# Three jobs of w_down's partial sums in DRAM get later places in the plan of the weights

## The chip, the cores and the metric

The kernel runs on one core of one Trainium2 chip. The metric is the device time of one execution in microseconds (us), lower is better. Three executions of the kernel before gave 869.16 to 869.73 us, median 869.48. A fourth execution was profiled and took 867.14 us; the trace in it spans 865.4 us from the first to the last instruction. All times "at" some microsecond are counted from the start of that span.

## What is computed

One encoder layer on 512 tokens of width 1024, in float32. Shortened:

```
n    = rms_norm(x);  proj = n @ w_in          # u | zu | zv | gate_a | gate_b
ga, gb = sigmoid(gate_a), sigmoid(gate_b)
ya   = s5(u); ya = ya * sigmoid(ya @ w_glu)   # bidirectional state-space scan
yb   = gelu(zu) * spatial_mix(layer_norm(gelu(zv)))
h    = x + (ga * (ya @ w_proj_a) + gb * (yb @ w_proj_b)) @ w_out
h    = h + cross_attention(rms_norm(h), rms_norm(mem); w_q, w_k, w_v, w_xo)
h    = h + (silu(f @ w_gate) * (f @ w_up)) @ w_down      # f = rms_norm(h)
out  = rms_norm(h)
```

## The kernel before

**Products.** Every float32 operand is split into a rounded high part and a remainder, and a product is three matmuls (high by high, high by low, low by high). The split of a weight block is one cast on ScalarE (`whi`, L85) and one subtraction on VectorE (`wlo`, L86). The tiles `whi` and `wlo` have three buffers each, and so has `raw`, into which SyncE loads a block from DRAM.

**Seven products for eight.** The matrices of the second gate (gb), of w_q, w_gate, w_up and w_down are cut into 2 by 2 quarters, and seven products of sums of quarters replace eight products of quarters. The products are numbered 1 to 7. The sums of weight quarters are made in three ways. For the second gate they are formed in SBUF, in the tile `gw`: loads by SyncE, additions on VectorE, and additions by transfers that GpSimd issues with `accum_op=ALU.add` (L261, L267). For w_q and w_down they are prepared in DRAM, in `qsum` and `dsum`: a *job* is a copy of one block of the weight into `dsum`, issued by SyncE (L316), and the addition of a second block onto it, issued by GpSimd (L317). There are 32 jobs: 0 to 7 for w_q, 8 to 31 for w_down. Jobs 8 to 13 are the six chunks of product 5's sum. `dsum` is read only at the end of the kernel (L330), and as the second operand of later jobs.

**The plan.** `plan` is the list of all weight blocks in the order in which the matmuls use them. Around the change its entries are: 28 to 35 w_proj_b; 36 to 49 the second gate, fourteen products in the order of `ORDER` (two column halves i = 0 and 1: 1, 1, 2, 2, 5/0, 6/0, 5/1, 7/0, 6/1, 4/0, 7/1, 3/0, 4/1, 3/1, written as product/half); 50 and 51 w_glu; 52 to 55 w_proj_a; 56 to 63 w_out; 64 to 71 w_k. `next_w` is called once for each entry, right before its matmuls are written down. At entry i it issues the loads of later entries, each with its own lead (`LOADS` = 3 entries for most), and the splits of entries up to i + 2. A job is hung on two entries: its copy on entry j and its addition on entry j + step, both with a lead of 0, so that they are written down when `next_w` reaches these entries.

**The order in the queues** is not the order in which the instructions are written down. A scheduling pass at build time simulates the kernel and lays out a fixed queue for each engine; at run time each queue is worked off in order, and an instruction that waits holds up those behind it. `tc.keep_in_program_order` (L316) binds an instruction to come somewhere behind the one that was written down for the same engine just before it. The copies of the jobs carry it, the additions don't. So the copy of the job at place 50 comes behind the load of entry 52, and the copy at place 52 behind the last of the four loads of `gat` (L1452), which are written down between w_glu and w_proj_a.

**The second gate, half 0, where it touches `gw`** (`plan_gates`, lines 233 to 270). The tile t of half 0 holds the operand of products 5 and 6; when product 6 has been split (cast and subtraction read t), GpSimd issues `t += b(1, 0)` (L261), and the result is the operand of product 4. The PSUM bank gx takes products 1, 6, 7 and 4 of a half, one onto the other, and is read out after 1, 6, 7 and 4; the read-out after 7 is `kept(gx[i], "u3")`, a copy on ScalarE (L1313). So product 4 of half 0 waits for the cast and the subtraction of its weights, and for that copy.

```
elif q == 6:
    nc.vector.tensor_tensor(b11, t, b11, ALU.subtract)
    nc.gpsimd.dma_start(t, b(1, 0), accum_op=ALU.add)
```

Of the kernel before, what the change touches and what calls it, by code (L numbers as in the profile page):

```python
# [52 lines left out]
def hybrid_layer_kernel(  # L53
# [160 lines left out]
    def query_block(i, j, n):  # L214
        return block(w_q, i * KD // 2, KD // 2, 512 * n + 256 * j, 256)
# [78 lines left out]
    def down_block(i, jc, c):  # L294
        row, k = (4 * c + 2 * i, 2) if c < CHUNKS - 1 else (NF - 2 + i, 1)
        return block(w_down, row, k, 512 * (1 - jc), 512)

    def down_sum(q, c):
        return dsum[q][:, 2 * c:min(2 * c + 2, NF // 2), :]

    def plan_sums(places):


        jobs = []
        for q, first, more in ((5, (0, 0), lambda n: query_block(0, 1, n)), (7, (0, 1), lambda n: query_block(1, 1, n)),
                               (6, None, lambda n: query_block(1, 1, n)), (4, None, lambda n: query_block(1, 0, n))):
            for n in range(2):
                jobs.append((qsum[q, n], qsum[q + (-1 if q == 6 else 2), n] if first is None else query_block(*first, n),
                             more(n)))
        for q, i, jc, more in ((5, 0, 0, lambda c: down_block(0, 1, c)), (7, 0, 1, lambda c: down_block(1, 1, c)),  # L310
                               (6, 1, 1, lambda c: down_sum(5, c)), (4, 1, 0, lambda c: down_sum(6, c))):
            for c in range(CHUNKS):
                jobs.append((down_sum(q, c), down_block(i, jc, c), more(c)))
        assert len(jobs) == len(places)
        for (dst, src, more), (j, step) in zip(jobs, places):
            plan[j][1].append((0, lambda d=dst, x=src: tc.keep_in_program_order(nc.sync.dma_start(d, x))))  # L316
            plan[j + step][1].append((0, lambda d=dst, x=more: nc.gpsimd.dma_start(d, x, accum_op=ALU.add)))  # L317
# [44 lines left out]
    for i in range(4):  # L362
# [4 lines left out]
    plan_down(w_down, lambda q, c: down_tokens[0](q, c), down_plan)  # L367
    plan_units(UNITS, down_plan)

    plan_sums([(5 + 3 * i, 3) for i in range(8)] + [(50 + 2 * i, 2) for i in range(7)] +  # L370
              [(85 + 3 * i, 3) for i in range(3)] + [(122 + 5 * i, 4) for i in range(14)])
    used_w = [0]

# [1661 lines left out]
```

## Time and profile before

| | |
|---|---|
| median of three executions | 869.48 us (869.16 to 869.73) |
| the profiled execution | 867.14 us |
| its span | 865.4 us |
| mean granted TensorE clock | 0.996 |
| DMA | 155.40 MB in 110135 packets |

In rows of a timeline the columns are start, length, engine, line of the kernel, operation, output<-inputs, how many, and in brackets how long the engine stood idle before and what ended that. "SPq" is SyncE's queue, PE is TensorE, DVE VectorE, ACT ScalarE, POOL GpSimd. In rows of windows each engine has its busy time and its count of instructions; then come the granted TensorE clock, the mean busy share of the 16 DMA engines and GB/s. In rows of DMA issues the last number is the time from issue to landing.

### The profile page before, as it was taken

The page shows a single profiled execution, that of the slowest core. Times are in us where ns is not written, and L with a number is a line of the kernel's source. Part 1 is how long each engine was busy: PE and PEld are TensorE (multiplying, and loading weights), DVE is VectorE, ACT ScalarE, POOL GpSimd, SP SyncE. Part 2 cuts the span into 40 slices and gives each one's busy share as a digit, 9 for nine tenths or more (in the row PEclk, how much of TensorE's full clock was granted, in tenths as well). Part 3 has the DMA queues.
Part 4 walks back from the last instruction along what each step waited for, and adds up shares of the span by engine and source line. Part 5 has one row for each costly group of instructions (what it writes and reads, how often), then busy time and mean ns, then how long its engine had stood idle before and what let it go on. Part 6 is the DMA issues. An engine that isn't in the chain of part 4 may idle for free.

```text
span 865.4 us, 14842 instructions
## 1 busy us (share of the span) xinstructions
PE 853.9 (99%) x5898; PEld 761.9 (88%) x5898; DVE 648.2 (75%) x890; ACT 475.1 (55%) x703; POOL 103.5 (12%) x157
## 2 busy tenths in 40 slices
PE   9999999999999899999999999999999999999996
PEld 6788888878889888889899888999999999988885
DVE  6699589957947658669658646767877768899876
ACT  6645774377436534557547544645545555656664
POOL 1001144100611010110010001001111111000000
PEclk9999999999999999999999999999999999999999
DMA  8559279645638586944687144557799789686641
GB/s 260 159 144 240 81 204 267 147 122 162 167 98 226 136 224 202 287 116 169 200 269 216 68 145 105 146 140 177 172 224 230 204 208 240 178 243 203 196 158 48
DMA packets 110135, 155.40 MB, mean 180 GB/s; under 512 B 8985, under 2 KB 77105, under 8 KB 110002
## 3 DMA queue, kind: packets, MB, share of 16 engines
q1 hardware_dynamic: 91762, 128.27, 45.3%
q0 software_dynamic: 18016, 25.66, 18.4%
q8 instruction: 46, 0.75, 0.3%
q10 hardware_dynamic: 288, 0.52, 0.2%
q14 instruction: 23, 0.19, 0.1%
HBM read 148.70 MB, written 37.20 MB: 215 GB/s over the span
## 4 chain that ended last, share of the span: by engine, by line
PE 96%; ACT 1%; DVE 1%; issue 1%; POOLq 0%; POOL 0%; ACTq 0%
PE pf L404 25%; PE pt L404 18%; PE px L1304 13%; PE dx L404 6%; PE pq L1304 6%; PE dq L404 3%; PE pv L1304 3%; PE gx L1304 3%; PE qx L1304 3%; PE dv L404 2%; PE ptr L577 1%; PE psc L404 1%; PE gq L1304 1%; PE po L404 1%; PE py L1093 1%; PE qq L1304 1%
## 5 line engine op out<-in xcount | busy, mean ns | idle before, releaser
L85 ACT CAST whi<-wraw 128x1024 fp32r<-128x1024 f32 x132 | 135.8, 1029 | 143.3 <-PE pf L404 37.2
L86 DVE TENSOR_TENSOR wlo<-wraw,whi 128x1024 fp32r<-128x1024 f32 x132 | 157.5, 1194 | 66.0 <-ACT whi L85 65.7
L404 PE MATMUL pf<-xn,whi 128*128 128x512 f32 x320 | 100.4, 393 | 0.0
L1304 PE MATMUL px<-fn,whi 128*128 128x256 f32 x480 | 83.3, 276 | 0.0
L1304 PEld LDWEIGHTS px<-fn,whi 128*128 128x128 f32 x480 | 72.5, 188 | 0.2
L404 PEld LDWEIGHTS pf<-xn,whi 128*128 128x128 f32 x320 | 59.6, 188 | 12.6 <-issue 0.5
L85 ACT CAST whi<-b 128x1024 fp32r<-128x1024 f32 x40 | 42.1, 1054 | 51.5 <-PE px L1304 26.3
L86 DVE TENSOR_TENSOR wlo<-b,whi 128x1024 fp32r<-128x1024 f32 x40 | 48.9, 1224 | 27.9 <-ACT whi L85 27.9
L1304 PE MATMUL px<-fn,wlo 128*128 128x256 f32 x240 | 66.4, 277 | 0.0
L404 PE MATMUL pf<-xn,wlo 128*128 128x512 f32 x160 | 62.9, 393 | 0.0
L1304 PE MATMUL pq<-s,whi 128*128 128x256 f32 x320 | 55.0, 276 | 0.0
L404 PE MATMUL dx<-whi,s 128*128 128x512 f32 x170 | 53.0, 390 | 0.0
L86 DVE TENSOR_TENSOR wlo<-t,whi 128x1024 fp32r<-128x1024 f32 x30 | 36.7, 1225 | 19.3 <-ACT whi L85 19.3
L85 ACT CAST whi<-t 128x1024 fp32r<-128x1024 f32 x30 | 31.6, 1052 | 35.2 <-PE pv L1304 12.6
L1304 PEld LDWEIGHTS pq<-s,whi 128*128 128x128 f32 x320 | 48.2, 188 | 0.0
L1304 PEld LDWEIGHTS px<-fn,wlo 128*128 128x128 f32 x240 | 45.1, 188 | 0.0
L1304 PE MATMUL pq<-s,wlo 128*128 128x256 f32 x160 | 44.2, 276 | 0.0
L404 PE MATMUL pt<-whi,xn 128*128 128x512 f32 x120 | 40.1, 402 | 0.0
L404 PEld LDWEIGHTS dx<-whi,s 128*128 128x128 f32 x170 | 31.8, 188 | 6.7 <-DVE s L86 0.3
L317 POOL DMA_DIRECT2D dsum<-in_w_down_dram x12 | 13.3, 1108 | 192.1 <-DMA dsum<-in_w_down_dram 192.1
L404 PEld LDWEIGHTS pf<-xn,wlo 128*128 128x128 f32 x160 | 30.1, 188 | 6.1 <-issue 0.2
L404 PE MATMUL dx<-wlo,s 128*128 128x512 f32 x85 | 33.0, 390 | 0.1
(485 smaller groups left out, 2340.0 us busy)
## 6 DMA issues: line engine op xcount, KB each, us to landing
wraw<-in_w_in_dram SPq DMA_DIRECT2D x34, 512.0 KB, 6.1
dsum<-in_w_down_dram SPq DMA_DIRECT2D x20, 512.0 KB, 6.4
wraw<-dsum SPq DMA_DIRECT2D x20, 512.0 KB, 3.7
b<-in_w_gate_dram SPq DMA_DIRECT2D x15, 512.0 KB, 5.1
b<-in_w_up_dram SPq DMA_DIRECT2D x15, 512.0 KB, 5.2
wraw<-in_w_down_dram SPq DMA_DIRECT2D x15, 512.0 KB, 4.7
dsum<-in_w_down_dram POOLq DMA_DIRECT2D x10, 512.0 KB, 7.3
dsum<-dsum POOLq DMA_DIRECT2D x10, 512.0 KB, 7.1
```

The costliest lines, as they stand in the source:

```text
L85: hi = nc.scalar.copy(dst_hi, src)
L86: lo = nc.vector.tensor_tensor(dst_lo, src, dst_hi.bitcast(F32), ALU.subtract)
L317: plan[j + step][1].append((0, lambda d=dst, x=more: nc.gpsimd.dma_start(d, x, accum_op=ALU.add)))
L404: last_mm[0] = nc.tensor.matmul(ps, a[x], b[y], start=start and i == 0, stop=stop and i == 2, skip_group_check=free)
L577: tr = nc.tensor.transpose(ps[:, j, :], src[:, k * P:(k + 1) * P], ident)
L1093: in_order(nc.tensor.matmul(ps[64 * j:64 * j + 64, :], a, b, start=g % 4 == k == 0, stop=k == 2, tile_position=(0, 64 * j), skip_group_che ...
L1304: nc.tensor.matmul(ps[:, j, :], a[x], b[y], start=start and j == k == i == 0, stop=k == 3 and i == 2, skip_group_check=True)
```

## The change

The places of jobs 8 to 14 are written out instead of computed. The step to the addition stays 2.

```diff
-    plan_sums([(5 + 3 * i, 3) for i in range(8)] + [(50 + 2 * i, 2) for i in range(7)] +
+    plan_sums([(5 + 3 * i, 3) for i in range(8)] + [(j, 2) for j in (53, 54, 55, 56, 58, 60, 62)] +
               [(85 + 3 * i, 3) for i in range(3)] + [(122 + 5 * i, 4) for i in range(14)])
```

Jobs 8, 9 and 10 (chunks 0, 1 and 2 of product 5's sum) go from places 50, 52 and 54 to 53, 54 and 55, their additions from 52, 54 and 56 to 55, 56 and 57. Jobs 11 to 14 keep 56, 58, 60 and 62. What is computed is the same.

## The prediction

> **What bounds the kernel now.** I read the page first, then the waits of TensorE, then the timelines of the engines around its one long wait.
>
> ```profile
> PE 853.9 (99%) x5898; PEld 761.9 (88%) x5898; DVE 648.2 (75%) x890; ACT 475.1 (55%) x703; POOL 103.5 (12%) x157
> ```
>
> TensorE is busy for 853.9 of 865.4 us. An edit that changes no arithmetic can only give back what TensorE waits, or what it loses at a lower clock. All its waits are these, from the view of waits:
>
> ```profile
> PE gx L1304 <- ACT u L1313: 2.4, 1, 2.4
> PE idle L612 <- DVE level L880: 1.1, 1, 1.1
> PE pt L483 <- ACT whi L656: 1.0, 1, 1.0
> PE pf L404 <- DVE yb_lo L86: 0.2, 1, 0.2
> ```
>
> L612, L483 and the yb_lo wait lie in code far ahead of the moved places. The first, half of the total, lies in the second gate. The timelines of TensorE, ScalarE, GpSimd and VectorE there:
>
> ```profile
> 284.21 0.28 PE L1304 MATMUL gx<-gse,wlo 128*128 128x256 f32 x1
> 286.93 0.39 PE L1304 MATMUL gx<-xn,whi 128*128 128x256 f32 x1 [2.45 <-ACT u L1313]
> ```
>
> ```profile
> 277.32 0.58 ACT L1404 COPY u<-gx 128x512 f32<-128x512 f32 x1
> 284.40 1.99 ACT L85 CAST whi<-gw 128x1024 fp32r<-128x1024 f32 x2 [6.51 <-PE gx L1304]
> 286.30 0.58 ACT L1313 COPY u<-gx 128x512 f32<-128x512 f32 x1
> ```
>
> ```profile
> 272.63 1.20 POOL L317 DMA_DIRECT2D dsum<-in_w_down_dram  x1 [31.20 <-DMA dsum<-in_w_down_dram]
> 273.99 1.35 POOL L261 DMA_DIRECT2D gw<-in_w_in_dram  x1 [0.16 <-issue]
> 278.96 1.28 POOL L261 DMA_DIRECT2D gw<-in_w_in_dram  x1 [3.62 <-DVE wlo L86]
> ```
>
> ```profile
> 270.65 2.40 DVE L86 TENSOR_TENSOR wlo<-gw,whi 128x1024 fp32r<-128x1024 f32 x2
> ...
> 277.44 1.23 DVE L86 TENSOR_TENSOR wlo<-gw,whi 128x1024 fp32r<-128x1024 f32 x1 [0.39 <-ACT whi L85]
> ```
>
> And the view of DMA issues in three narrow windows, at 215.8 (an earlier addition onto gw, L267, with GpSimd's queue of transfers empty), at 273.99 and at 278.96:
>
> ```profile
> gw<-in_w_in_dram POOLq DMA_DIRECT2D x1, 512.0 KB, 6.1
> ```
>
> ```profile
> gw<-in_w_in_dram POOLq DMA_DIRECT2D x1, 512.0 KB, 10.3
> ```
>
> ```profile
> gw<-in_w_in_dram POOLq DMA_DIRECT2D x1, 512.0 KB, 7.9
> ```
>
> TensorE waits from 284.49 (284.21 + 0.28) to 286.93 for the copy of u on ScalarE, which ends at 286.88. That copy reads the result of product 7, but it stands third in ScalarE's queue, behind two casts that start at 284.40. The row blames gx of TensorE for the 6.51 us before them. I don't follow it. The first of the two casts makes the weights of product 4 of half 0 from `gw`, and the addition that completes them, the first row of L261, landed at 273.99 + 10.3 = 284.3. The second addition landed at 278.96 + 7.9 = 286.9, after both casts had begun, so it can't be the one.
>
> So the late thing is the first L261, for two reasons. It was issued late: GpSimd stood for 31.20 us at the addition of a job, waiting for its copy, and L261 came 0.16 us after that addition had been issued. And it took 10.3 us behind the job's 512 KB in GpSimd's one queue of transfers, against 6.1 alone.
>
> **Which job that is.** SyncE's queue:
>
> ```profile
> 265.00 1.49 SPq L1452 DMA_DIRECT2D gat<-gad  x1
> 266.53 0.60 SPq L316 DMA_DIRECT2D dsum<-in_w_down_dram  x1
> ...
> 296.97 0.37 SPq L141 DMA_DIRECT2D wraw<-in_w_proj_a_dram  x1
> 297.39 0.58 SPq L316 DMA_DIRECT2D dsum<-in_w_down_dram  x1
> 299.44 6.02 SPq L141 DMA_DIRECT2D wraw<-in_w_proj_a_dram  x3
> 310.39 0.37 SPq L141 DMA_DIRECT2D wraw<-in_w_out_dram  x1
> 310.81 0.56 SPq L316 DMA_DIRECT2D dsum<-in_w_down_dram  x1
> ...
> 315.82 0.37 SPq L141 DMA_DIRECT2D wraw<-in_w_out_dram  x1
> 317.68 0.34 SPq L525 DMA_DIRECT2D g_x<-in_xattn_norm_g_dram  x1
> 318.06 0.56 SPq L316 DMA_DIRECT2D dsum<-in_w_down_dram  x1
> ```
>
> A copy is bound behind what was written down for SyncE just before it. Job 8 (place 50) is bound to the load of entry 52, the first of w_proj_a: the copy at 297.39. Job 9 (place 52) is bound to the last `gat`, and these loads are hoisted far ahead: the copy at 266.53, right behind it. So job 9, not job 8, reaches into the gate. Job 10 (bound to the load of entry 56) is the copy at 310.81, job 11 the one at 318.06.
>
> **The change part by part.** *Copies.* Job 8 at place 53 is bound to the load of entry 55, the last of w_proj_a, which ends at 305.46 (299.44 + 6.02). Job 9 at 54 is bound to the load of entry 56 (310.39), job 10 at 55 to that of 57 (315.82). No job is bound to `gat` any more, and nothing of L316 can come into SyncE's queue ahead of 305.46. Each copy costs 0.56 to 0.60 us of that queue. Behind the load of 55 it stands idle until 310.39; behind that of 56 the present job 10 has the same place; behind that of 57 there are 1.49 us (316.19 to 317.68). All three fit: 0 us. Without that cover a load behind them would come 0.6 us later.
>
> *Additions.* Each takes 1.20 us of GpSimd and follows its copy. Behind 305.46 they come after both L261. L261 then waits only for the subtraction that reads t, the first of the two at 270.65, which ends at 271.85. The second L261 shows the lag: 277.44 + 1.23 = 278.67, issued at 278.96, 0.29 later. So the first is issued at 272.14 instead of 273.99, **1.85 us earlier**.
>
> *Landing.* The trace has no transfer of this kind at this place with the queue empty. Bounds: 6.1 us (alone) and 10.3 us (itself, with the job's transfer ahead). I take 7.9, since the second L261 shared the engines with the end of the first, as the first will with other loads. It lands at 280.0 (bounds 278.2 and 282.4). When must it? From the first cast's start to the end of u's copy ScalarE needs 286.88 - 284.40 = 2.48 us, and TensorE comes free at 284.49: until 282.0. At 280.0 **the whole wait of 2.45 us goes**; at the upper bound 0.6 us of it stay (2.45 - 1.85).
>
> *Clock.* Two windows behind the wait (the granted clock is the third figure from the end):
>
> ```profile
> 288.20:291.70 3.50, 3.50 (x19) 3.50 (x18) 1.97 (x3) 1.19 (x3) 0.00 (x0) 0.51 0.25 80
> 291.70:300.00 8.30, 8.30 (x72) 8.30 (x72) 6.06 (x8) 4.73 (x7) 0.00 (x0) 1.00 0.31 99
> ```
>
> For 3.5 us after the wait the granted clock is 0.51. The loss is 0.49 x 3.50 = **1.7 us**. Bounds: 0, if the dip is not due to the wait, and 1.7. I take 1.7, because the dip begins 1.3 us after the only wait of such length, and because the clock is 1.00 after it. The Trainium skill, "TensorE: Matmul & The Clock Gate", section "HAM oscillation — how this bites in real kernels", speaks against this: by it TensorE's clock is cut by idle gaps over about 3.4 us, and this gap is 2.45. By that rule the dip would be no part of the gain; it is a rival below.
>
> *What is late next.* Product 4 of half 1, from the second L261. In the chain of waits it starts here:
>
> ```profile
> 297.18 2.86 PE gx L1304 x24
> ```
>
> 4.2 us earlier that is 293.0. Its weights land by 286.9 and need a cast and a subtraction, 1.05 (the cast of this kind takes 0.95 to 1.05) and 1.23 us: 289.2, 3.8 us of room.
>
> *The stage that gets the jobs.* Between 297 and 330 jobs 8, 10 and 11 are issued now; job 9 is added, two transfers of 512 KB.
>
> ```profile
> 310.00:320.00 10.00, 10.00 (x46) 8.29 (x45) 6.94 (x8) 3.80 (x6) 1.14 (x1) 1.00 0.75 245
> 320.00:330.00 10.00, 10.00 (x46) 8.29 (x45) 6.31 (x9) 3.40 (x5) 1.13 (x1) 1.00 0.76 196
> ```
>
> At 196 GB/s, the slower of these, 1.05 MB are 5.4 us of the DMA engines; in the 25 us from 305 to 330, at a share of about 0.75, some 6 us are free. TensorE is fully busy here and waits for nothing. So 0 us; the upper bound is 5.4 us, if all of it fell on a load that TensorE waits for (870.7 in the end, counted with the slower case below), and no gain is to be had, as there is no wait to shorten. I take 0, since the work fits into the free share.
>
> **Sum** against the profiled execution's own 867.14: -2.45 - 1.7 = -4.2, that is 862.9. The three runs shown have their median 2.34 us above it, 869.48, and I carry that difference over: **865.3 us**.
>
> **Rivals.**
>
> *The wait goes only in part, or the dip stays.* If the transfer still takes 10.3 us, 1.85 us are gained and 0.6 of waiting stays: 867.6 with the dip, 865.9 without. If the wait goes and the dip stays, as the skill's rule would have it: 2.45 gained, 867.0. For it: the transfer also shared the engines with other loads. Against: any transfer of up to 9.8 us (272.14 to 282.0) takes the whole wait away, and the dip stands right behind the wait.
>
> *The change doesn't do what it says:* 869.5. Either the 6.51 us were TensorE's after all, as the row says, or the scheduling pass, whose queues are laid out anew, puts one new wait of the same size elsewhere. For it: few waits are left because the order happens to fit, and any moved transfer shifts the simulated times behind it. Against: the sum 273.99 + 10.3 meets the cast's start to 0.1 us.
>
> *Slower: GpSimd's waiting moves to the norm of mem.* Three rows of GpSimd, VectorE and TensorE:
>
> ```profile
> 347.07 0.56 POOL L548 TENSOR_TENSOR r<-ms,mhalf 128x1 f32<-128x1 f32 x1 [5.24 <-DVE ms L547]
> 353.16 1.16 POOL L317 DMA_DIRECT2D dsum<-in_w_down_dram  x1 [5.53 <-DMA dsum<-in_w_down_dram]
> ```
>
> ```profile
> 347.67 0.75 DVE L563 SCALAR_TENSOR_TENSOR mt<-mt,r,g_mem 128x512 f32<-128x512 f32 x1 [0.69 <-POOL r L548]
> ```
>
> ```profile
> 352.28 0.60 PE L577 MATMUL ptr<-ident,mt 128*128 128x128 f32 x4
> ```
>
> If the new order puts the addition at 353.16 ahead of r, r starts at 354.3 instead of 347.07, 7.2 us late. On VectorE the scaling of mt waits for r, and everything queued behind it waits too; on TensorE the transposes of mt wait for the scaling. It ends at 348.42 now, 3.9 us ahead of the transposes at 352.28, so the stall is between 3.3 us, by the transposes, and 7.2, if something in VectorE's queue is needed without delay; I take the middle, 5.3, and 1.7 for a new dip: -4.2 + 7.0 = +2.8, **872.3**. It is slower from the point where such a stall exceeds 2.5 us (4.2 - 1.7). For it: the four additions now follow each other closely in this queue. Against: the job at 353.16 (place 58) is not moved, and r stands ahead of it now; the additions of jobs 8 to 11 end near 330, as the last of them still follows the copy at 318.06.
>
> **How the numbers follow.** Forecast 0.63, with a range of its own from 864.4 to 866.6; the partial case 0.13 (to 867.6); no effect 0.14; slower 0.10. A measurement of this kernel can tell about 0.2%, 1.7 us, from no change, so the first two are faster, 0.76, the third the same, 0.14, the last slower, 0.10. The first two hold too little for 8 in 10, so the range reaches into the third: 864.4 to 869.6.
>
> **What would show it.** Right: no addition of L317 between 240 and 300 in GpSimd's timeline; the first L261 near 272.1, landing 6 to 9 us later; ScalarE's two casts apart, the first near 280; no wait of gx in TensorE's list; a granted clock of 1.00 up to the end; copies of L316 behind the loads near 305, 311 and 316, each minus what was gained. Wrong: L261 early and landed early, and the cast still at 284.4 (then TensorE's row was right); a new wait in TensorE's list; r of L548 behind an addition.

## The result, and the profile after

| | before | after |
|---|---|---|
| median | 869.88 us (869.16 to 870.82, 6 runs) | 865.26 us (863.08 to 865.90, 6 runs) |
| profiled execution | 867.14 us | 864.86 us |
| its span | 865.4 us | 863.1 us |

TensorE's busy time on the page of after:

```profile
PE 854.4 (99%) x5898; PEld 762.3 (88%) x5898; DVE 647.5 (75%) x890; ACT 475.2 (55%) x703; POOL 103.5 (12%) x157
```

It is 854.4 of 863.1 us, where it was 853.9 of 865.4: the same instructions, with less time between them. The ratio on record is 0.9944, with a 95% interval from 0.9931 to 0.9957: faster by 0.56%. The medians differ by 4.6 us, the two profiled executions by 2.3 us only. The chain of waits of each shows where the rest went. Before:

```profile
278.88 5.50 PE gx L1304 x47
...
302.78 32.66 PE pf L404 x144
```

And after:

```profile
280.81 8.46 PE gx L1304 x72
...
300.51 32.66 PE pf L404 x144
```

Both pieces named gx begin with product 7 of half 0, and both pieces named pf with the first product behind the second gate. The way between them takes 23.90 us before and 19.70 after: **4.2 us less, the sum of the prediction**. From pf to the end of the span it is 562.6 us in both. But the profiled execution of after came to product 7 1.93 us later. That is a difference of the first 15 us, read here in one window of both. Before, then after (the granted clock is the third figure from the end):

```profile
7.45:14.27 6.82, 5.81 (x32) 4.07 (x30) 5.89 (x11) 5.32 (x11) 0.55 (x1) 1.00 1.05 351
```

```profile
7.45:14.27 6.82, 6.17 (x20) 4.58 (x19) 5.27 (x9) 4.01 (x9) 0.95 (x1) 0.50 1.07 357
```

At half the clock TensorE got through 20 matmuls in place of 32. The change touches nothing there, and in the other kernels below product 7 begins anywhere from 278.9 to 282.4 us. So times in the gate are compared counted from product 7. One of all the executions told of below, of the kernel with more work at the start, was granted a clock of 0.556 throughout, took 1435.54 us and is left out.

The waits of TensorE after:

```profile
PE idle L612 <- DVE level L880: 1.1, 1, 1.1
PE pt L483 <- ACT whi L656: 0.6, 1, 0.6
PE pf L404 <- DVE yb_lo L86: 0.2, 1, 0.2
```

The wait of gx, 2.4 us before, is gone, and no new one stands in the list. GpSimd's timeline, the issue of the first L261, VectorE's and ScalarE's timelines:

```profile
239.43 4.22 POOL L975 DMA_DIRECT2D tt<-kd  x8 [1.65 <-DMA kd<-ks]
274.94 1.37 POOL L261 DMA_DIRECT2D gw<-in_w_in_dram  x1 [31.29 <-issue]
280.90 1.31 POOL L261 DMA_DIRECT2D gw<-in_w_in_dram  x1 [4.59 <-DVE wlo L86]
308.86 1.16 POOL L317 DMA_DIRECT2D dsum<-in_w_down_dram  x1 [26.65 <-DMA dsum<-in_w_down_dram]
...
344.92 0.56 POOL L548 TENSOR_TENSOR r<-ms,mhalf 128x1 f32<-128x1 f32 x1 [5.37 <-DVE ms L547]
350.90 1.16 POOL L317 DMA_DIRECT2D dsum<-in_w_down_dram  x1 [5.42 <-DMA dsum<-in_w_down_dram]
```

```profile
gw<-in_w_in_dram POOLq DMA_DIRECT2D x1, 512.0 KB, 6.0
```

```profile
272.57 2.40 DVE L86 TENSOR_TENSOR wlo<-gw,whi 128x1024 fp32r<-128x1024 f32 x2
274.89 0.68 DVE L1379 TENSOR_TENSOR part<-part,gs 128x512 f32<-128x512 f32 x1
```

```profile
281.00 1.05 ACT L85 CAST whi<-gw 128x1024 fp32r<-128x1024 f32 x1 [1.18 <-DMA gw<-in_w_in_dram]
283.86 1.05 ACT L85 CAST whi<-gw 128x1024 fp32r<-128x1024 f32 x1 [1.81 <-PE gx L1304]
284.82 0.58 ACT L1313 COPY u<-gx 128x512 f32<-128x512 f32 x1
```

No addition of a job stands between the batch of tt and the two L261. The first lands at 274.94 + 6.0 = 280.9, and the cast follows at 281.00. The two casts that stood together at 284.40 are now 1.8 us apart, and the copy of u, third behind them, finds its product when it gets to run. The norm r at 344.92 still stands ahead of the addition at 350.90.

The gate's stretch and SyncE's queue behind it:

```profile
280.90:300.40 19.50, 19.50 (x169) 19.50 (x168) 13.14 (x15) 11.37 (x15) 1.30 (x1) 1.00 0.50 124
```

```profile
294.69 8.49 SPq L141 DMA_DIRECT2D wraw<-in_w_proj_a_dram  x4
303.23 0.61 SPq L316 DMA_DIRECT2D dsum<-in_w_down_dram  x1
308.11 0.38 SPq L141 DMA_DIRECT2D wraw<-in_w_out_dram  x1
308.54 0.58 SPq L316 DMA_DIRECT2D dsum<-in_w_down_dram  x1
...
313.96 0.57 SPq L316 DMA_DIRECT2D dsum<-in_w_down_dram  x1
```

TensorE is busy for all of the 19.50 us, at a clock of 1.00. The copies of jobs 8, 9 and 10 come right behind the loads of entries 55, 56 and 57.

### The profile page after: what moved, and what is told of

Its sections match the earlier page's. It is cut to its first block, busy times and chain, and to the rows that moved or that the text cites. A ratio compares the mean times of both kernels' runs of the same rounds, so it can differ in the third digit from the quotient of the medians.

```text
span 863.1 us, 14838 instructions
## 1 busy us (share of the span) xinstructions
PE 854.4 (99%) x5898; PEld 762.3 (88%) x5898; DVE 647.5 (75%) x890; ACT 475.2 (55%) x703; POOL 103.5 (12%) x157
## 4 chain that ended last, share of the span: by engine, by line
PE 95%; ACT 1%; DVE 1%; DMA 1%; issue 1%; SPq 0%; POOLq 0%; POOL 0%; ACTq 0%
PE pf L404 25%; PE pt L404 18%; PE px L1304 13%; PE dx L404 6%; PE pq L1304 6%; PE dq L404 3%; PE pv L1304 3%; PE gx L1304 3%; PE qx L1304 3%; PE dv L404 2%; PE ptr L577 1%; PE psc L404 1%; PE po L404 1%; PE py L1093 1%; PE qq L1304 1%; PE gq L1304 1%
```

## The experiments

"Start" is the start of product 7 of half 0, "gate" the time from there to the first pf, both read from TensorE's timeline. The profiled time is that of the execution that was traced; where more were timed, the median follows, and the ratio on record to the kernel before on the same chip, with its 95% interval (it is not the quotient of the two medians).

| kernel | profiled | start | wait of gx | gate | median; ratio |
|---|---|---|---|---|---|
| before | 867.14 | 278.95 | 2.45 | 23.67 | 869.88 |
| after | 864.86 | 280.88 | none | 19.47 | 865.26; 0.9944 [0.9931, 0.9957] |
| job 9 alone moved | 864.87 | 280.94 | none | 19.47 | 864.87; 0.9962 [0.9941, 0.9983] |
| jobs 8 and 10 alone | 869.79 | 281.50 | 2.47 | 23.64 | 867.49; 0.9994 [0.9978, 1.0011] |
| addition bound | 865.50 | 281.60 | none | 19.47 | 864.86; 0.9958 [0.9942, 0.9975] |
| two jobs in the gate | 872.36 | 281.43 | 4.94 | 26.47 | 872.79; 1.0050 [1.0030, 1.0069] |
| job between the two L261 | 863.08 | 278.91 | none | 19.47 | one execution |
| wait without transfer | 863.27 | 279.11 | none | 19.69 | one execution |
| transfer without wait | 867.76 | 279.12 | 3.00 | 24.12 | one execution |
| more work at the start | 866.61 | 282.41 | none | 19.47 | 864.87; 0.9955 [0.9938, 0.9973] |
| after, again | 865.82 | 281.80 | none | 19.47 | 865.42; 0.9959 [0.9943, 0.9975] |
| before, again (1) | 869.49 | 281.41 | 2.35 | 23.52 | one execution |
| before, again (2) | 867.10 | 279.29 | 1.86 | 23.08 | one execution |
| before, again (3) | 865.60 | 279.06 | 2.06 | 21.81 | one execution |

The first four experiments have 20 runs of before beside them, with a median of 867.56 us; the two with more work at the start and after again have 21, with 867.85. The three kernels with one execution each have one of before, 865.15 us, and before again has one, 869.85; against the spread of the starts a single time says little, and these kernels are read by their gate.

### Which of the three jobs

Job 9 alone, and then the other two alone:

```diff
-    plan_sums([(5 + 3 * i, 3) for i in range(8)] + [(50 + 2 * i, 2) for i in range(7)] +
+    plan_sums([(5 + 3 * i, 3) for i in range(8)] + [(j, 2) for j in (50, 53, 54, 56, 58, 60, 62)] +
```

> Only job 9 (the copy that stood right behind the last gat load) gets its later place, 53; jobs 8 and 10 stay at 50 and 54. Theory (GpSimd's queue: the addition of job 9 holds up the first addition onto gw, and its transfer goes ahead of it): the whole gain, 4.2 us off the run before, ratio about 0.995; no L317 on GpSimd between 240 and 300; no wait of gx on TensorE; the stretch from product 7 of half 0 to the first matmul of w_glu about 19.7 us, as after, against 23.9 before. Rival (what counts is that all three jobs leave, or the new order of the queues): the gain is less than half, ratio above 0.9975.

```diff
-    plan_sums([(5 + 3 * i, 3) for i in range(8)] + [(50 + 2 * i, 2) for i in range(7)] +
+    plan_sums([(5 + 3 * i, 3) for i in range(8)] + [(j, 2) for j in (53, 52, 55, 56, 58, 60, 62)] +
```

> Jobs 8 and 10 get their later places, 53 and 55; job 9 stays at 52. Theory: no gain, ratio 0.999 to 1.001, the wait of 2.4 us on gx and the half clock behind it are still there, the stretch is 23.9 us. Rival (spreading the traffic, or the new order): a part of the gain, ratio at or below 0.9975.

With job 9 alone moved the gate takes 19.47 us, to the hundredth what the whole change gives. With the other two moved it keeps its 23.64. The waits of TensorE and the timeline of GpSimd in the second kernel:

```profile
PE gx L1304 <- ACT u L1313: 2.5, 1, 2.5
```

```profile
275.05 1.20 POOL L317 DMA_DIRECT2D dsum<-in_w_down_dram  x1 [30.91 <-DMA dsum<-in_w_down_dram]
276.42 1.35 POOL L261 DMA_DIRECT2D gw<-in_w_in_dram  x1 [0.16 <-DVE part L1379]
```

They are the rows of before, 2.4 us later, where the start is 2.55 us later. So one of the three moves is the change; the other two cost nothing and bring nothing.

### The addition or the copy

The plan of before, but with the addition of job 9 (and no other) held in the program's order, so that it can't be hoisted ahead of the gate; its copy stays where it was.

```diff
-        for (dst, src, more), (j, step) in zip(jobs, places):
+        for n, ((dst, src, more), (j, step)) in enumerate(zip(jobs, places)):
+            bound = tc.keep_in_program_order if n == 9 else lambda x: x
...
-            plan[j + step][1].append((0, lambda d=dst, x=more: nc.gpsimd.dma_start(d, x, accum_op=ALU.add)))
+            plan[j + step][1].append((0, lambda d=dst, x=more, b=bound: b(nc.gpsimd.dma_start(d, x, accum_op=ALU.add))))
```

> All places as before; only the addition of job 9 is bound to come behind what was written down for GpSimd just before it, so behind both additions onto gw. Its copy still runs at 266.5 inside the gate. Theory (it is the addition in GpSimd's queue): the whole gain, ratio about 0.995, stretch about 19.7 us. Rival (the copy's traffic on the 16 engines, or its 0.6 us in SyncE's queue): no gain, ratio 0.999 to 1.001.

Again 19.47 us, with the 512 KB of the copy still moving through the gate. GpSimd's queue there:

```profile
275.67 1.37 POOL L261 DMA_DIRECT2D gw<-in_w_in_dram  x1 [31.17 <-issue]
281.62 1.31 POOL L261 DMA_DIRECT2D gw<-in_w_in_dram  x1 [4.58 <-DVE wlo L86]
```

What has to leave is the addition, not the traffic of the copy.

### Twice the cause

Jobs 8 and 9 both at place 52, so that both are bound to the last `gat`:

```diff
-    plan_sums([(5 + 3 * i, 3) for i in range(8)] + [(50 + 2 * i, 2) for i in range(7)] +
+    plan_sums([(5 + 3 * i, 3) for i in range(8)] + [(j, 2) for j in (52, 52, 54, 56, 58, 60, 62)] +
```

> Jobs 8 and 9 both at place 52, so two copies stand behind the last gat load and two additions ahead of the first addition onto gw. Theory: the first L261 is issued some 3 us later than before and has 1 MB ahead of it instead of 0.5, so it lands 6 to 7 us later; the wait of 2.4 us grows to 8 or 9 us, the half clock behind it to between 3.4 and 7 us: 876 us, ratio 1.006 to 1.01. Rival (TensorE's row is right, the casts wait for gx and not for the transfer): no change, ratio 0.999 to 1.001.

Slower, at 1.005. The waits of TensorE, and GpSimd:

```profile
PE gx L1304 <- ACT u L1313: 4.9, 1, 4.9
```

```profile
274.65 1.20 POOL L317 DMA_DIRECT2D dsum<-in_w_down_dram  x1 [30.31 <-DMA dsum<-in_w_down_dram]
277.06 1.17 POOL L317 DMA_DIRECT2D dsum<-in_w_down_dram  x1 [1.20 <-issue]
277.77 1.82 POOL L261 DMA_DIRECT2D gw<-in_w_in_dram  x1
```

The direction is right: two additions ahead of the first L261, and twice the wait. The size was expected too large, 8 to 9 us of waiting and 876 us. Counted from product 7, L261 was issued only 1.3 us later than before, not some 3, and it landed 11.5 us after its issue, 1.2 more than before's 10.3: 2.5 us later in all, where 6 to 7 were expected. The first of the two additions had been issued 3.1 us ahead of it (274.65 to 277.77), so a part of its transfer was over by then. The gate takes 26.47 us, 7.0 more than after: 4.94 of waiting, and the rest at half a clock, which here lasts 6.83 us (289.19 to 296.02), of which TensorE worked 4.1.

### A job in the gate, but not ahead of the first L261

Job 9's copy at place 38 and its addition held in order between the two L261, with the `bound` of the experiment before last:

```diff
-    plan_sums([(5 + 3 * i, 3) for i in range(8)] + [(50 + 2 * i, 2) for i in range(7)] +
+    plan_sums([(5 + 3 * i, 3) for i in range(8)] + [(50, 2), (38, 4)] + [(50 + 2 * i, 2) for i in range(2, 7)] +
```

> Job 9 stays in the gate, but GpSimd never waits for it there: its copy goes to place 38, ahead of the gat loads, and its addition is bound between the first and the second addition onto gw. Theory (only what stands ahead of the first L261 costs): the first L261 lands about 6 us after its issue, no wait of gx on TensorE, stretch 19.5 us; the second L261 has 512 KB ahead of it and lands 8 to 10 us after its issue, still ahead of its product. Rival (any job's traffic inside the gate costs): a wait of 1 us or more on gx, stretch above 20.5 us.

The gate takes 19.47 us and gx waits for nothing: the second L261 then lands 7.6 us after its issue (8 to 10 were expected), and has the room for it. It is the order that costs, not the job's being there. Its one time, 863.08 us, is also the lowest of after, and it had an early start (278.91), so it isn't a faster version.

### The wait or the transfer

The prediction gave two reasons for the late landing: L261 was issued late, as GpSimd stood at the addition, and it took long, behind that addition's 512 KB. These two kernels set the two apart. In the first, 64 KB of job 9's addition stay ahead of L261 and wait for the copy as before; the other 448 KB come later.

```diff
+            if n == 9:
+                plan[j + step][1].append((0, lambda d=dst[:, :, 0:64], x=more[:, :, 0:64]: nc.gpsimd.dma_start(d, x, accum_op=ALU.add)))
+                plan[57][1].append((0, lambda d=dst[:, :, 64:512], x=more[:, :, 64:512]: tc.keep_in_program_order(nc.gpsimd.dma_start(d, x, accum_op=ALU.add))))
+                continue
```

> All places as before. Of job 9's addition one eighth (64 KB) stays in its place ahead of the first L261 and waits for the copy as before; the other 448 KB are bound behind job 10's addition. So GpSimd's wait stays and most of the transfer ahead goes. If the transfer ahead is the cause: L261 is issued as late as before and lands about 6.5 us after it, no wait on gx, stretch 19.5 us. If the late issue is the cause: the wait of 2.4 us stays, stretch 23.7 us.

In the second the copy is long done (place 38), and the whole addition is held right ahead of the first L261, behind a small product that makes GpSimd start there when the split of product 6 is ready.

```diff
-                    nc.gpsimd.dma_start(t, b(1, 0), accum_op=ALU.add)
+                    if i == 0:
+                        stamp = np_.tile([P, 1], F32, tag="ms", name="stamp", bufs=2)
+                        nc.gpsimd.tensor_tensor(stamp, ops[1][:, 0, 0:1].bitcast(F32), mhalf, ALU.mult)
+                        late_add[0]()
+                        tc.keep_in_program_order(nc.gpsimd.dma_start(t, b(1, 0), accum_op=ALU.add))
+                    else:
+                        nc.gpsimd.dma_start(t, b(1, 0), accum_op=ALU.add)
```

> The complement: job 9's copy goes to place 38 and has landed long before; its whole addition is bound right ahead of the first L261, and a one-column multiplication on GpSimd that reads the split of product 6 keeps it from being issued earlier than L261 could be. So GpSimd waits for no copy, but 512 KB go ahead in its queue of transfers. If the transfer ahead is the cause: L261 lands about 10 us after its issue, a wait of 2 to 3 us on gx, stretch 22.5 to 24.5 us. If the late issue by GpSimd's wait is the cause: no wait, stretch 19.5 us.

The wait without the transfer: GpSimd, the issue of L261, ScalarE.

```profile
272.80 1.20 POOL L318 DMA_DIRECT2D dsum<-in_w_down_dram  x1 [30.64 <-DMA dsum<-in_w_down_dram]
274.16 1.35 POOL L261 DMA_DIRECT2D gw<-in_w_in_dram  x1 [0.16 <-issue]
```

```profile
gw<-in_w_in_dram POOLq DMA_DIRECT2D x1, 512.0 KB, 7.8
```

```profile
282.07 2.00 ACT L85 CAST whi<-gw 128x1024 fp32r<-128x1024 f32 x2 [4.01 <-PE gx L1308]
```

The transfer without the wait: GpSimd, the issue of L261, the waits of TensorE.

```profile
272.13 1.14 POOL L264 TENSOR_TENSOR stamp<-wlo,mhalf 128x1 f32<-128x1 f32 x1 [30.00 <-DVE wlo L86]
273.21 1.20 POOL L325 DMA_DIRECT2D dsum<-in_w_down_dram  x1
273.97 1.82 POOL L266 DMA_DIRECT2D gw<-in_w_in_dram  x1
```

```profile
gw<-in_w_in_dram POOLq DMA_DIRECT2D x1, 512.0 KB, 11.1
```

```profile
PE gx L1314 <- ACT u L1323: 3.0, 1, 3.0
```

L261 is issued at 274.16 and 273.97, both within 0.2 us of before's 273.99, and their starts differ by 0.01 us. With 64 KB ahead it lands after 7.8 us (6.5 were expected), and the gate takes 19.69 us, 0.2 more than after. With 512 KB ahead it lands after 11.1, and the gate takes 24.12. So at the same issue time it is the size of the transfer ahead in GpSimd's queue that makes the wait. The late issue was not run quite alone: the 64 KB still add 1.8 us to the 6.0 of after. Together the two use up the room (L261 lands at 281.96, the two casts stand together again) and cost 0.2 us. With nothing ahead, an L261 issued at 274.16 would have landed near 280.2 (an estimate, with the 6.0 of after).

### The clock: at the start, and behind the wait

The runs of one kernel lie in groups. To see whether more work at the start brings all runs into the lowest group, three matmuls of no use were added shortly ahead of a gap of TensorE, near 9.5 us, with after itself beside it:

```diff
-        idles(3)
+        idles(6)
```

> The changed kernel with three more matmuls of no use (idles(6) instead of idles(3) behind the first transposes), so that TensorE is busier between 7.5 and 10.1 us, where it waits 0.65 us for the first split weights and where the traces show a half clock in some executions and a full one in others. Theory (the first microseconds' clock, not the change, makes the runs of one kernel differ by up to 2.7 us): no half clock behind 7.4 us in the profile, the gate starts near 279.0, and the times of its runs lie closer together, near 863.3. Rival (the three matmuls only delay what stands behind them, and the clock falls by when its windows begin): the gate starts between 279 and 282 as before, times spread from 863 to 866, perhaps 0.5 us later. In both the stretch of the gate stays 19.5 us and gx waits for nothing.

> The changed kernel itself once more, on the same chip as the one with more work at the start, so that the two have the same runs of the kernel before beside them. Expected: times from 863.0 to 865.9, a median near 864.9, the stretch of the gate 19.5 us, no wait of gx, and a start of the gate anywhere from 278.9 to 281.6 us.

The rival holds: the start came at 282.41 us, and ten runs of this kernel go from 863.04 to 866.61 us. After itself goes from 863.13 to 865.82. The added matmuls only cost their own time.

Then the kernel before was profiled three more times.

> The kernel before, profiled again. Its times lie in three groups, near 865.3, 867.4 and 869.8 us. If the half clock behind the wait always comes with the wait, only the start can make the difference and no execution could be below 867.1 less what a faster start than 278.95 us leaves. If it comes only in some executions, one near 865.3 has the wait of 2.45 us and no half clock behind it (stretch of the gate near 21.9 us), and one near 869.8 has a late start and the half clock (23.7 us).

> The kernel before, once more: as for the first of these looks. Wait of gx 2.45 us in each; the stretch of the gate 23.7 us with a half clock behind the wait, 21.9 without.

> The kernel before, once more: as for the first of these looks. Wait of gx 2.45 us in each; the stretch of the gate 23.7 us with a half clock behind the wait, 21.9 without.

They fell into all three groups. The waits are 2.35, 1.86 and 2.06 us, each shorter than the 2.45 expected. The second and the third start within 0.23 us of each other and have a wait each, but the half clock follows only in the second. Windows of TensorE in the second: the 3.41 us that end where the lower clock begins, and the 3.41 us behind them (the first figure after the length is what TensorE was busy):

```profile
283.96:287.37 3.41, 1.55 (x13) 1.35 (x12) 2.13 (x2) 3.21 (x4) 0.00 (x0) 1.00 0.66 107
287.37:290.78 3.41, 3.41 (x18) 3.41 (x17) 2.56 (x4) 1.33 (x3) 0.00 (x0) 0.50 0.12 8
```

In all traces the changes of the granted clock lie whole steps of 3.413 us apart (in the second of these three it rose at 10.89 and fell at 287.37, 81 steps later). In the third it fell only at the end, at 861.94 us, after the last matmul; 169 steps back from there lies 285.08:

```profile
285.08:288.50 3.42, 1.84 (x15) 1.84 (x16) 3.29 (x4) 3.26 (x6) 0.00 (x0) 1.00 0.21 34
288.50:291.90 3.40, 3.40 (x30) 3.40 (x30) 2.46 (x3) 1.88 (x3) 0.00 (x0) 1.00 0.42 127
858.60:861.90 3.30, 0.00 (x0) 0.00 (x0) 0.84 (x2) 0.72 (x1) 0.55 (x1) 1.00 0.71 271
861.95:863.80 1.85, 0.00 (x0) 0.00 (x0) 0.00 (x0) 0.00 (x0) 0.00 (x0) 0.50 0.20 74
```

And in the execution of before that the prediction read:

```profile
284.85:288.26 3.41, 1.33 (x11) 1.33 (x12) 2.78 (x3) 3.41 (x5) 0.00 (x0) 1.00 0.35 56
```

The clock fell after windows in which TensorE was busy for 1.33 and 1.55 us, and did not after one with 1.84. The wait of the third, 2.06 us, was longer than the second's 1.86, but 0.48 of it lay in the window ahead. The four other traces with a wait agree: 1.23 us busy in the first of these three, 1.08 with jobs 8 and 10 alone, 1.18 with two jobs in the gate, 0.69 in the transfer without wait, and half a clock behind each. The gate without the half clock takes 21.81 us, 2.3 more than after; with it 23.08 to 23.67.

The start does not fit this reading. In the profiled execution of after the clock fell at 7.45 us, behind a window in which TensorE was busy all the time:

```profile
4.03:7.45 3.42, 3.42 (x16) 1.90 (x16) 1.18 (x5) 1.48 (x5) 0.55 (x1) 1.00 0.86 265
```

For 1.98 us of it TensorE ran four matmuls whose operand is one row (L638); whether such matmuls count as less work was not tried. What followed went with the work in the next window, at half a clock: with 2.76 us busy in after the next one was at half a clock too, with 3.03 in the wait without transfer it was at the full one.

## Why the prediction was right

**What is late.** Right. The first L261 was it, and neither the second nor TensorE's product named by the row for the 6.51 us: with it landing at 280.9 the cast follows 0.1 us later, in every kernel above in which it comes late the casts follow it, and binding one addition moves it all.

**Which job.** Right: job 9 alone has the whole gain, jobs 8 and 10 none.

**The issue, 1.85 us earlier: mis-sized.** In before's time it came at 274.94 - 1.93 = 273.01, 0.98 us earlier than 273.99, not at 272.14. The prediction let it follow the first of the two subtractions. That one begins at 272.57 and takes 1.23, so it ends at 273.80, and the issue came 1.14 us behind it, not the 0.29 taken from the second L261. By the trace it was not the end of the second subtraction that released it, as that came at 274.97 (272.57 + 2.40), after the issue. The time is the same in all of them: the issue came 0.05 us after the 274.89 at which VectorE's next instruction begins, and 0.04 to 0.06 after that instruction in every other kernel in which no addition stands ahead. In the kernel with the transfer without wait, the small product that reads the first subtraction's result began at 272.13, 0.08 after that subtraction ended. What the DMA's issue did in the 1.14 us is not shown.

**The landing, 7.9 us: mis-sized the other way.** It took 6.0, as it did alone. Both errors together put it at 280.9 - 1.93 = 279.0 instead of 280.0, on the same side of the deadline.

**The deadline at 282.0.** Right, and seen from its edge: the wait without transfer lands at 281.96 with a start 0.16 us later, and the gate grows by 0.2 us.

**Two reasons for the late landing.** Both were real, but unequal, and the prediction did not weigh them. At the old issue time a landing after 10.3 or 11.1 us makes the wait; one after 7.8 us does not. By the measured terms, as estimates, since neither was run alone, the earlier issue gives 273.01 + 10.3 = 283.3, 1.3 us past the deadline, the partial case; the shorter transfer gives 273.99 + 6.0 = 280.0, which is in time.

**The clock, 1.7 us.** Right for the execution it was read from: 4.20 us of gate, of which 2.45 were waiting. The rule of the Trainium skill ("TensorE: Matmul & The Clock Gate", section "HAM oscillation — how this bites in real kernels"), that only gaps over some 3.4 us matter, does not hold here: gaps of 1.86, 2.35 and 2.45 us were followed by a half clock of 3.4 us. But the loss is not in every execution: before again (3) has the wait without it. The gain of one execution is therefore 2.3 us or 3.6 to 4.2.

**The jobs' new stage and what is late next, 0 us.** Right in sum: from pf to the end it is 562.73 us after and 562.76 before. Not for want of contention: the load of w_out at 313.55 took 8.8 us to land where that at 315.82 took 4.2 before. TensorE still waited for none. The next late thing, the second L261, landed at 280.90 + 6.0 = 286.9 and was not waited for.

**The median, 865.3.** Met by 865.26, with some luck. The prediction took the 2.34 us between its execution and the three runs as something the change keeps. The three runs were not traced; that they had the late start is argued from before again (1), which at 869.49 us started 2.46 us later. By its times after has the late start in most runs too (864.80 to 865.90 us; one at 863.08). On the two chips with 20 and 21 runs of before its medians were 867.56 and 867.85 us, with runs down to 864.93 and 865.27, and the ratios of the same effect are 0.996 there instead of 0.994. Which start a run gets differs from execution to execution on one chip; why the six runs of before beside this result were all slow starts, if they were, was not tried.

## What to carry to other kernels

A queue that one engine fills and that runs in order makes every transfer pay for what was put ahead of it: find the transfer that a cast or a product follows at once, and see what stands ahead of it there, above all work that a scheduling pass has hoisted and nobody needs soon. Binding that one transfer behind the urgent one is enough; here one of three moves did all. Before dividing two medians, look at where in the span the executions part: here up to 2.7 us of spread came from the first 15 us, more than half the effect that was measured.

## What the runs showed of the hardware

- The lower clock comes in pieces of 3.41 us, on a grid that lies differently in each execution. In the gate it went with how much TensorE worked in one piece of the grid (0.69 to 1.55 us of 3.41 in six executions: half clock next; 1.84 in one: full), not with how long the wait was. That the bound is half a piece, 1.71 us, would fit but is not proved, and the start has a fall behind a piece of full work (4.03 to 7.45 us in after) that this doesn't explain.
- The same grid makes the start: TensorE has its full clock from 4.96 us up to the gate in the execution of before that the prediction read, and only from 12.65 us in before again (1), where product 7 starts 2.46 us later.
- The first L261, 512 KB added from DRAM onto a tile by GpSimd's queue, took 5.9 to 6.2 us from issue to landing with nothing ahead, 7.8 with 64 KB, 10.2 to 11.1 with 512 KB and 11.5 with two such ahead. An addition of a job is not free in the background: 512 KB issued 0.8 to 1.4 us ahead made L261 take some 4 to 5 us longer. Whether a plain copy in that queue would cost as much was not tried.
